# Softmax maxima in the score product: four rows spread by VectorE, or one row transposed per head and copied by ScalarE

## The chip, the cores and the metric

The kernel runs on one core of a Trainium2 chip, in float32 throughout. The time is the device time of one launch, in microseconds (us). Before the change three runs took 1527.92, 1532.71 and 1538.26 us; the median is 1532.71. "Faster" or "slower" is said against runs of the unchanged kernel on the same chip.

## The reference

Two layers over 1024 latent tokens (a grid of 16 rows by 64 columns) and 256 context tokens, width 1024. Layer 0 holds two attentions side by side, each with 8 query heads of width 64 that share 2 key/value heads: one global (every query sees the 256 context and 1024 latent keys), one windowed (context and latent keys at a distance of at most 128) with a learned sink logit per head. Layer 1 holds a convolution branch and a neighbourhood attention: 8 heads, each latent query sees the context and a window of 8 by 16 grid cells, with a table of biases. Gates, projections, norms and modulation stand around them. What matters here is the softmax:

```python
def gqa_attend(q, k, v, bias=None, sink=None):
    s = jnp.einsum("bqhgd,bkhd->bhgqk", q, k, preferred_element_type=jnp.float32) * ATTN_SCALE
    if bias is not None:
        s = s + bias
    if sink is not None:
        sink_col = jnp.broadcast_to(sink.astype(jnp.float32)[None, :, :, None, None], s.shape[:-1] + (1,))
        p = jax.nn.softmax(jnp.concatenate([s, sink_col], axis=-1), axis=-1)[..., :-1]
    else:
        p = jax.nn.softmax(s, axis=-1)
    return jnp.einsum("bhgqk,bkhd->bqhgd", p.astype(v.dtype), v)
```

## The kernel before

**Split numbers.** A float32 operand of a large product is held as a high part in the fast float32 format (`fp32r`) and a low part, the rest. A projection is three products (high by high, high by low, low by high; `mm3`, lines 351 to 354). The splitting is a cast on ScalarE (line 331) and a subtraction on GpSimd or VectorE (line 334).

**Attention by groups.** A group is 512 query columns: in layer 0 the four query heads of one key/value head for one block of 128 queries (40 groups, 20 of them windowed, with sinks), in layer 1 one head's 512 queries of half the grid, in four blocks of 128 (16 groups). Scores are computed with keys on the partitions and queries along the free axis, one tile of 128 keys by up to 512 queries at a time, into one of two PSUM banks `st`:

- line 529: keys' high and low parts (128 rows, `KA`) by the queries' high part, stored twice (`QH`);
- line 533: the keys' high part (64 rows of `KB`) by the queries' low part (64 rows of `QL`), and in the same contraction four more rows. Rows 64 to 67 of `KB` hold 1.0 (memset on GpSimd, lines 404 and 603). Rows 64 to 67 of `QL` hold minus the maximum of each query: row 64 + j has the values of head (or block) j in that head's 128 columns and zeros elsewhere. So the product subtracts each query's maximum from all its scores.

ScalarE then takes the exponential from the bank (line 541; in layer 1, where a bias is first added by VectorE in line 538, line 539), casts it to a high part (331), GpSimd or VectorE makes the low part (334), and three products per tile add up the values and the denominators in the bank `ov` (lines 480 to 482). These run three tiles behind the scores. For groups with a sink a last product (line 485) adds the sink's share of the denominator from further rows of `QL`.

**The maxima.** They are found ahead, with queries on the partitions: products `mx` (lines 643, 655, 663; in layer 1, 1405 and 1413) into one of two banks, each reduced by VectorE (645, 656, 664, 1407, 1414) into `mp`. `attn_prep` ends with `nmt`, 128 queries by 4 maxima; with a sink there are 12 columns: 4 maxima, and 4 high and 4 low parts of the sinks' exponentials (lines 433 to 446).

**The step of the change**, `attn_fin` (lines 450 to 461), brings `nmt` into `QL`. TensorE transposes it (line 457) into a bank `mx`, so that it is 4 (or 12) rows by 128 queries. VectorE (line 458) reads each row four times over, once for each head's columns, and multiplies by a constant matrix `bd` (12 by 4: −1 on the diagonal of the first four rows, +1 on those of the other eight), into rows 64 to 67 (or 75) of `QL`.

**What sets the order.** Each engine works through its own queue in order. The order is laid out when the program is built: the framework follows the order of the code with priorities and an estimated timeline (`schedule_with_timeline_sim=True`). The code is a set of generators: `attn_gen` yields between tiles, and while a group's tiles run, the next group's `attn_fin` and the preparation of the one after are stepped along (lines 507 to 515, 547 and 552). `weave` (line 562) puts steps of other work, projections of later heads and the output projections, between those steps. The transposition is pinned behind the last score product issued so far (`issue_after(sts[-1].ins)`, line 456). Bank `mx` is shared by turns: the transposition takes the next of the two, and the maxima's product two turns later must wait until the transposed rows have been read.

Of the kernel before, what the change touches and what calls it, by code (L numbers as in the profile page):

```python
# [10 lines left out]
F32 = mybir.dt.float32  # L11
F32R = mybir.dt.float32r
ALU = mybir.AluOpType
# [5 lines left out]
P = 128  # L19
# [70 lines left out]
def tile_kernel(ctx: ExitStack, tc: tile.TileContext, a, out):  # L90
# [14 lines left out]
    def bank(tag, name):  # L105
        if tag == "pp" and solo[0]:
            turn[0] += 1
            tag = ("pp", "mx")[turn[0] // 2 % 2]
        return ps.tile([P, 512], F32, tag=tag, name=name, bufs=BUFS[tag])
# [3 lines left out]
    def nm(s):  # L113
        uid[0] += 1
        return f"{s}_{uid[0]}"
# [5 lines left out]
    def const(name, shape, eng=SY, pool=None):  # L121
        t = (pool or cp).tile(shape, F32, tag=name, name=name)
        eng.dma_start(t, a[name])
        return t
# [265 lines left out]
        VE.scalar_tensor_tensor(dst, dst, 1.0, psrc, op0=ALU.add, op1=ALU.mult)  # L390


    bd = const("k_bd", [12, 4], SC)
    Ks, Vs = [], []

    def v_tiles(pool, n, bufs=1):
# [4 lines left out]
    def k_tiles(pool, hi, n, bufs=1):  # L401
        KB = pool.tile([P, n * P], F32R, tag="KB", name=nm("KBt"), bufs=bufs)
        KA = hi.tile([P, n * P], F32R, tag="KA", name=nm("KAt"), bufs=bufs)
        GP.memset(KB[64:68, :].bitcast(F32), 1.0)
        Ks.append((KA, KB))

    def load_k(k, kh, kl):
# [42 lines left out]
    def attn_fin(g):  # L450

        nr, nmt, QL = g.nr, g.nmt, g.QL
        for _ in range(FIN[layer[0]]):
            yield
        tr2 = bank("mx", nm("trn"))
        with tc.issue_after(sts[-1].ins) if sts else ExitStack():
            PE.transpose(tr2[0:nr, 0:P], nmt[:, 0:nr].bitcast(F32), ident)
        VE.tensor_tensor(QL[64 : 64 + nr, :].rearrange("p (h q) -> p h q", h=4),
                         tr2[0:nr, None, 0:P].broadcast_to([nr, 4, P]),
                         bd[0:nr, :, None].broadcast_to([nr, 4, P]), op=ALU.mult)  # L460
        yield

    def attn_gen(pool, groups, vshare, look, nexts=None):

        preps = [g.prep for g in groups]
        items = [(g, t) for g in groups for t in range(len(g.tiles))]
        pend = []
        cnt = [0]

        def flush():  # L470
            g, t, ph, pl = pend.pop(0)
            k, q0, n, _ = g.tiles[t]
            if t == 0:
                g.ov = bank("ov", nm("ov"))
                if g.load_v is not None:
                    g.load_v()
            V = g.v(k)
            last = t == len(g.tiles) - 1
            o = g.ov[:, q0 : q0 + n]
            PE.matmul(o, V[:, 64:192], ph[:, :n], start=(t == 0), stop=False)  # L480
            PE.matmul(g.ov[0:64, q0 : q0 + n], V[:, 0:64], ph[:, :n], start=False, stop=False)  # L481
            PE.matmul(o, V[:, 64:192], pl[:, :n], start=False, stop=(last and g.sink is None))  # L482
            if last:
                if g.sink is not None:
                    PE.matmul(g.ov, g.skm(), g.QL[0:76, :], start=False, stop=True)
                r1 = pool.tile([P, 8, 32], F32, tag="r1", name=nm("r1"), bufs=1)
                r8 = pool.tile([P, 8], F32, tag="r8", name=nm("r8"), bufs=2)
                rb = pool.tile([P, 256], F32, tag="rb", name=nm("rb"), bufs=1)
                for e in range(2):
                    VE.transpose(r1[e * 64 : (e + 1) * 64].rearrange("p a b -> p (a b)")  # L490
                                 .rearrange("p (a q) -> p a q", a=2), g.den(g.ov[64:128, :], e))
                VE.reciprocal(r8, r1[:, :, 0])
                VE.transpose(rb, r8[:, :, None].broadcast_to([P, 8, 32]))
                g.finish(g.ov, rb)

        if layer[0]:
            for g in groups[:3]:
                queries(g, kvs[-1])
        for p in preps[:2]:
            for n_, _ in enumerate(p):  # L500
                if n_ % 2:
                    yield
        for _ in attn_fin(groups[0]):
            pass
        if layer[0]:
            groups[0].copy()
        for gi, g in enumerate(groups):
            ids = [gi + 2] if gi + 2 < len(groups) else []
            if nexts is not None and gi in nexts:
                ids = nexts[gi]  # L510
            nx = [preps[k] for k in ids]
            if gi + 1 < len(groups):
                nx.insert(1 if ids[:1] == [gi + 1] else 0, attn_fin(groups[gi + 1]))
            g.next = chain.from_iterable(nx)
            g.step = -(-(18 * len(ids) + 4) // len(g.tiles))
        for g, t in items[:AHEAD]:
            g.ahead(t)
        for x, (g, t) in enumerate(items):
            if x + AHEAD < len(items):
                items[x + AHEAD][0].ahead(items[x + AHEAD][1])  # L520
            if t == 0:
                g.start()
                if layer[0] and g.no + 3 < len(groups):
                    queries(groups[g.no + 3], kvs[-1])
            k, q0, n, extra = g.tiles[t]
            KA, KB = g.k()
            st = bank("st", nm("st"))
            cs = slice(k * P, (k + 1) * P)
            sts.append(PE.matmul(st[:, :n], KA[:, cs], g.QH[:, q0 : q0 + n], start=True, stop=False))  # L529
            if not g.bias:  # L530
                for lhs, rhs in extra():
                    PE.matmul(st[:, :n], lhs, rhs, start=False, stop=False)
            PE.matmul(st[:, :n], KB[0:68, cs], g.QL[0:68, q0 : q0 + n], start=False, stop=True)  # L533
            ph = pool.tile([P, 512], F32R, tag="ph", name=nm("ph"), bufs=look + 1)
            pl = pool.tile([P, 512], F32R, tag="pl", name=nm("pl"), bufs=look + 1)
            pf = pool.tile([P, 512], F32, tag="pf" if layer[0] else "ost", name=nm("pf"), bufs=PFB)
            if g.bias and extra is not None:
                VE.tensor_tensor(pf[:, :n], st[:, :n], extra(), op=ALU.add)
                acts.append(SC.activation(pf[:, :n], pf[:, :n], AF.Exp))
            else:  # L540
                acts.append(SC.activation(pf[:, :n], st[:, :n], AF.Exp, scale=1.0 if g.bias else SCALE))  # L541
            cnt[0] += 1
            split(pf[:, :n], ph[:, :n], pl[:, :n], "s", "v" if cnt[0] % vshare == 0 else "g")
            pend.append((g, t, ph, pl))
            if t == len(g.tiles) // 2:
                g.gate()
            for _ in range(g.step // 2):
                next(g.next, None)
            yield
            if len(pend) > look:  # L550
                flush()
            for _ in range(g.step - g.step // 2):
                next(g.next, None)
            if t == len(g.tiles) - 1:
                for _ in g.next:
                    pass
            yield
        while pend:
            flush()
            yield  # L560
# [39 lines left out]
    def kv_tiles():  # L600

        KB = a0.tile([P, NTOK], F32R, tag="KB", name=nm("KBt"), bufs=1)
        GP.memset(KB[64:68, :].bitcast(F32), 1.0)
        for _ in range(2):
            KA = a0.tile([P, NTOK], F32R, tag="KA", name=nm("KAt"), bufs=2)
            V = a0.tile([P, 10, 192], F32R, tag="V", name=nm("Vt"), bufs=2)
            GP.memset(V[:, :, 128:192].bitcast(F32), 1.0)
            KV.append((KA, KB, V))
# [107 lines left out]
    with ExitStack() as p0x:  # L716
# [99 lines left out]
            VE.tensor_copy(gain5[:, 4, :], gain[:, 64:128])  # L816
            bmask = const("k_bm", [P, 384], SY, a0)
        bmt = a0.tile([P, 2, P], F32R, tag="bmt", name="bmt")
        sk = a0.tile([76, P], F32R, tag="sk", name="sk")
        cst = a0.tile([P, 512], F32, tag="ost", name="cst", bufs=2)  # L820
        with after_mod(4):
            SY.dma_start(cst[:, 0:256], a["k_bt"].rearrange("p a b -> p (a b)"))
            SY.dma_start(cst[0:76, 256:384], a["k_sk"])
        VE.tensor_copy(bmt, cst[:, 0:256].rearrange("p (a b) -> p a b", a=2))
        VE.tensor_copy(sk, cst[0:76, 256:384])

        tails = []
        beat = [0]
# [787 lines left out]
def _consts():  # L1616
# [16 lines left out]
    nxt = np.where(kk <= q, f(0), neg)  # L1633
    k["k_bm"] = np.concatenate([prev, z, nxt], 1).astype(f)
    k["k_bt"] = np.ascontiguousarray(np.stack([prev.T, nxt.T], 1)).astype(f)
    k["k_bd"] = np.where(np.arange(12)[:, None] < 4, f(-1), f(1)) * (np.arange(12)[:, None] % 4 == np.arange(4)[None, :])
    k["k_bd"] = k["k_bd"].astype(f)
    sk = np.zeros((76, 128), f)
    sk[68:76, 64:] = 1
    k["k_sk"] = sk  # L1640
    return k

# [92 lines left out]
```

## Time and profile before

| | |
|---|---|
| timed runs | 1527.92, 1532.71, 1538.26 us, median 1532.71 |
| span of the profiled execution, first to last instruction | 1528.5 us |
| TensorE products / weight loads busy | 1451.0 / 1167.2 us |
| VectorE / ScalarE / GpSimd busy | 1031.7 / 748.1 / 788.0 us |
| mean granted TensorE clock | 0.976 |
| instructions | 21545 |

The profiled execution is one more run; its own device time beyond its span is not recorded, and its span lies 4.2 us below the median of the timed runs. Its rows name an engine (PE is TensorE's products, PEld its weight loads, DVE VectorE, ACT ScalarE, POOL GpSimd, SP SyncE; a q behind it, as in ACTq, is the engine's sequencer, which issues DMAs), a line of the kernel, the operation, the tile written and the tiles read. In a row of one line or tile, the three numbers are the shortest, median and longest duration in ns, then the first and last start. In a row of order of time, the first number is the start in us, the second how long the run of equal instructions lasted, "x3" how many they are, and in brackets how long the engine had been idle and what released it. In a row of waits, the numbers are the total in us, how often, and the longest. In a row by stretches, each engine's busy time and its count of instructions follow, then the granted clock (1.00 is full), the share of the DMA engines' time and GB/s. Recorded ends of matrix products are modelled, and successive products overlap.

Layer 0's attention runs from about 146 to 886 us (windowed heads first), its output projection and the norms until 930, layer 1's convolution and projections to about 1200, its attention to 1476, the last projections and the norm to the end.

### The profile page before, as it was taken

How to read it: one execution, taken by the hardware profiler on the slowest of the kernel's cores; microseconds unless marked ns; L12 is line 12 of the kernel's file. 1: busy time of each engine (PE TensorE's matmuls, PEld its weight loads, DVE VectorE, ACT ScalarE, POOL GpSimd, SP SyncE). 2: the span in 40 equal slices, each digit the busy share in tenths (PEclk: the TensorE clock that was granted, in tenths of full speed). 3: DMA queues.
4: the chain of work that ended last, by engine and by line, in shares of the span. 5: the costliest groups of instructions: out<-in, count | busy, mean ns of one | idle time of the engine just before them, and what ended most of it. 6: DMA issues, size and time to landing. Idle time of an engine off the chain costs nothing.

```text
span 1528.5 us, 21545 instructions
## 1 busy us (share of the span) xinstructions
PE 1451.0 (95%) x7144; PEld 1167.2 (76%) x7144; DVE 1031.7 (67%) x2095; ACT 748.1 (49%) x1418; POOL 788.0 (52%) x628
## 2 busy tenths in 40 slices
PE   6999999998998999999999889999999999989996
PEld 2786877896896777886777568888887788868775
DVE  2643566589578856457676948899848666567766
ACT  3642433443435564447646665343334455455564
POOL 3360443555454766557645665665532434364665
PEclk9999999999999999999999999999999999989998
DMA  9564325422312246121202021210484677877642
GB/s 366 201 225 135 106 69 174 135 77 88 114 56 76 85 138 210 49 69 54 59 28 66 35 67 56 62 56 28 158 253 144 207 219 240 248 222 234 178 129 110
DMA packets 154167, 199.83 MB, mean 131 GB/s; under 512 B 14716, under 2 KB 95816, under 8 KB 154056
## 3 DMA queue, kind: packets, MB, share of 16 engines
q1 hardware_dynamic: 147392, 186.88, 38.9%
q10 hardware_dynamic: 6664, 11.57, 2.3%
q8 instruction: 56, 0.92, 0.3%
q14 instruction: 55, 0.45, 0.1%
HBM read 148.07 MB, written 49.02 MB: 129 GB/s over the span
## 4 chain that ended last, share of the span: by engine, by line
PE 79%; DVE 11%; issue 3%; DMA 3%; ACT 2%; POOL 1%; ACTq 0%; SPq 0%; DVEq 0%; POOLq 0%
PE p L352 6%; PE p L354 6%; PE p L353 6%; PE ov L480 5%; PE ov L482 4%; PE ov L481 4%; PE po L352 4%; PE st L533 4%; PE st L529 4%; PE po L353 4%; PE po L354 4%; PE pq L352 4%; PE pq L353 3%; PE pq L354 3%; PE pg L352 2%
## 5 line engine op out<-in xcount | busy, mean ns | idle before, releaser
L334 POOL TENSOR_TENSOR pl<-pf,ph 128x512 fp32r<-128x512 f32 (+4 forms) x321 | 394.0, 1239 | 384.9 <-ACT ph L331 337.3
L541 ACT ACTIVATE pf<-st 128x512 f32<-128x512 f32 x284 | 166.5, 597 | 203.6 <-PE st L533 165.2
L334 POOL TENSOR_TENSOR wl<-wr,wh 128x512 fp32r<-128x512 f32 (+2 forms) x131 | 169.3, 1302 | 136.5 <-ACT wh L331 124.0
L331 ACT CAST ph<-pf 128x512 fp32r<-128x512 f32 (+4 forms) x364 | 209.5, 588 | 27.1 <-PE ov L481 15.9
L352 PE MATMUL p<-hh,wh 128*128 128x512 f32 x448 | 176.0, 393 | 3.4 <-DVE spq L1233 1.3
L353 PE MATMUL p<-hl,wh 128*128 128x512 f32 x448 | 174.5, 390 | 0.0
L354 PE MATMUL p<-hh,wl 128*128 128x512 f32 x448 | 173.0, 391 | 0.0
L480 PE MATMUL ov<-ph,Vt 128*128 128x512 f32 (+4 forms) x364 | 141.0, 387 | 4.2 <-DVE y L693 2.0
L529 PE MATMUL st<-QH,KAt 128*128 128x512 f32 (+4 forms) x364 | 140.2, 386 | 3.9 <-ACT pf L541 3.1
L482 PE MATMUL ov<-pl,Vt 128*128 128x512 f32 (+4 forms) x364 | 141.1, 388 | 2.2 <-POOL pl L334 2.1
L481 PE MATMUL ov<-ph,Vt 128*64 128x512 f32 (+4 forms) x364 | 138.9, 381 | 0.0
L533 PE MATMUL st<-QL,KBt 68*128 68x512 f32 (+4 forms) x364 | 136.4, 386 | 0.9 <-issue 0.8
L1177 DVE SCALAR_TENSOR_TENSOR cps<-U,taps,cps 128x512 f32<-128x512 f32 x184 | 125.9, 748 | 0.7
L331 ACT CAST wh<-wr 128x512 fp32r<-128x512 f32 (+2 forms) x134 | 80.9, 613 | 84.1 <-PE po L353 15.9
L352 PEld LDWEIGHTS p<-hh,wh 128*128 128x128 f32 x448 | 84.2, 188 | 21.5 <-ACT spq L1231 1.6
L656 DVE TENSOR_REDUCE mp<-mx 128x1 f32<-128x512 f32 x128 | 85.3, 681 | 19.3 <-PE mx L655 18.3
L354 PEld LDWEIGHTS p<-hh,wl 128*128 128x128 f32 x448 | 84.1, 188 | 17.4
L353 PEld LDWEIGHTS p<-hl,wh 128*128 128x128 f32 x448 | 84.2, 188 | 17.1 <-issue 0.2
L1020 DVE SCALAR_TENSOR_TENSOR x<-po,modT,x 128x512 f32<-128x512 f32 (+1 forms) x72 | 46.9, 657 | 64.0 <-PE po L354 63.5
L352 PE MATMUL pq<-wh,hh 128*128 128x384 f32 x256 | 88.2, 344 | 1.0 <-ACT hh L331 1.0
L353 PE MATMUL pq<-wl,hh 128*128 128x384 f32 x256 | 87.3, 341 | 0.0
L354 PE MATMUL pq<-wh,hl 128*128 128x384 f32 x256 | 86.6, 342 | 0.0
(287 smaller groups left out, 3417.2 us busy)
## 6 DMA issues: line engine op xcount, KB each, us to landing
mw<-in_mod_w_dram SPq DMA_DIRECT2D x16, 1024.0 KB, 5.3
Q<-qs SPq DMA_DIRECT2D x40, 256.0 KB, 2.1
QH<-Q SPq DMA_DIRECT2D x80, 128.0 KB, 2.7
mw<-in_mod_w_dram SPq DMA_DIRECT2D x16, 512.0 KB, 6.8
wr<-in_od_d_dram SPq DMA_DIRECT2D x32, 256.0 KB, 3.1
wr<-in_ev_qkv_dram SPq DMA_DIRECT2D x16, 384.0 KB, 5.0
KAt<-KD SPq DMA_DIRECT2D x16, 384.0 KB, 6.5
wr<-in_od_wo_dram SPq DMA_DIRECT2D x22, 256.0 KB, 3.4
```

The lines of the kernel that those rows point to most:

```text
L331: acts.append(SC.copy(hi, src))
L334: (GP if leng == "g" else VE).tensor_tensor(lo, src, hi.bitcast(F32), op=ALU.subtract)
L352: PE.matmul(o, lh, rh, start=first, stop=False)
L353: PE.matmul(o, lh, rl, start=False, stop=False)
L354: last.append(PE.matmul(o, ll, rh, start=False, stop=end))
L480: PE.matmul(o, V[:, 64:192], ph[:, :n], start=(t == 0), stop=False)
L481: PE.matmul(g.ov[0:64, q0 : q0 + n], V[:, 0:64], ph[:, :n], start=False, stop=False)
L482: PE.matmul(o, V[:, 64:192], pl[:, :n], start=False, stop=(last and g.sink is None))
L529: sts.append(PE.matmul(st[:, :n], KA[:, cs], g.QH[:, q0 : q0 + n], start=True, stop=False))
L533: PE.matmul(st[:, :n], KB[0:68, cs], g.QL[0:68, q0 : q0 + n], start=False, stop=True)
L541: acts.append(SC.activation(pf[:, :n], st[:, :n], AF.Exp, scale=1.0 if g.bias else SCALE))
L1177: VE.scalar_tensor_tensor(pc, uc, w, pc, op0=ALU.mult, op1=ALU.add)
```

## The change

The maxima enter line 533 as one row: `KB` has a single row of −1.0 and `QL` a single row with all 512 maxima. To get them into one row, the four heads (or blocks) are transposed one at a time: four transpositions, each of the one column of `nmt` that belongs to the head (with a sink of three columns: maximum, high and low part of the sink's exponential, a step of four apart), each into its own 128 columns of the same bank. ScalarE copies the result, 1 row (or 3) by 512, into row 64 (or rows 64 to 66) of `QL`. The constant matrix and its DMA are gone; line 533 contracts over 65 rows, line 485 over 67, and the sink's constant matrix has 67 rows. All four transpositions are pinned behind the last score product, as the one was.

```diff
-    bd = const("k_bd", [12, 4], SC)
     Ks, Vs = [], []
...
     def k_tiles(pool, hi, n, bufs=1):
         KB = pool.tile([P, n * P], F32R, tag="KB", name=nm("KBt"), bufs=bufs)
         KA = hi.tile([P, n * P], F32R, tag="KA", name=nm("KAt"), bufs=bufs)
-        GP.memset(KB[64:68, :].bitcast(F32), 1.0)
+        GP.memset(KB[64:65, :].bitcast(F32), -1.0)
...
         tr2 = bank("mx", nm("trn"))
+        nr //= 4
         with tc.issue_after(sts[-1].ins) if sts else ExitStack():
-            PE.transpose(tr2[0:nr, 0:P], nmt[:, 0:nr].bitcast(F32), ident)
-        VE.tensor_tensor(QL[64 : 64 + nr, :].rearrange("p (h q) -> p h q", h=4),
-                         tr2[0:nr, None, 0:P].broadcast_to([nr, 4, P]),
-                         bd[0:nr, :, None].broadcast_to([nr, 4, P]), op=ALU.mult)
+            for h_ in range(4):
+                PE.transpose(tr2[0:nr, h_ * P : (h_ + 1) * P],
+                             nmt.rearrange("p (j h) -> p j h", h=4)[:, 0:nr, h_].bitcast(F32), ident)
+        SC.copy(QL[64 : 64 + nr, :], tr2[0:nr, :])
         yield
...
                 if g.sink is not None:
-                    PE.matmul(g.ov, g.skm(), g.QL[0:76, :], start=False, stop=True)
+                    PE.matmul(g.ov, g.skm(), g.QL[0:67, :], start=False, stop=True)
...
-            PE.matmul(st[:, :n], KB[0:68, cs], g.QL[0:68, q0 : q0 + n], start=False, stop=True)
+            PE.matmul(st[:, :n], KB[0:65, cs], g.QL[0:65, q0 : q0 + n], start=False, stop=True)
...
     def kv_tiles():
 
         KB = a0.tile([P, NTOK], F32R, tag="KB", name=nm("KBt"), bufs=1)
-        GP.memset(KB[64:68, :].bitcast(F32), 1.0)
+        GP.memset(KB[64:65, :].bitcast(F32), -1.0)
...
-        sk = a0.tile([76, P], F32R, tag="sk", name="sk")
+        sk = a0.tile([67, P], F32R, tag="sk", name="sk")
...
-            SY.dma_start(cst[0:76, 256:384], a["k_sk"])
+            SY.dma_start(cst[0:67, 256:384], a["k_sk"])
...
-        VE.tensor_copy(sk, cst[0:76, 256:384])
+        VE.tensor_copy(sk, cst[0:67, 256:384])
...
-    k["k_bd"] = np.where(np.arange(12)[:, None] < 4, f(-1), f(1)) * (np.arange(12)[:, None] % 4 == np.arange(4)[None, :])
-    k["k_bd"] = k["k_bd"].astype(f)
-    sk = np.zeros((76, 128), f)
-    sk[68:76, 64:] = 1
+    sk = np.zeros((67, 128), f)
+    sk[65:67, 64:] = 1
     k["k_sk"] = sk
```

## The prediction

> **What bounds the kernel now.** I read the page first: its busy line and its chain of waits.
>
> ```profile
> span 1528.5 us, 21545 instructions
> ...
> PE 1451.0 (95%) x7144; PEld 1167.2 (76%) x7144; DVE 1031.7 (67%) x2095; ACT 748.1 (49%) x1418; POOL 788.0 (52%) x628
> ...
> PE 79%; DVE 11%; issue 3%; DMA 3%; ACT 2%; POOL 1%; ACTq 0%; SPq 0%; DVEq 0%; POOLq 0%
> ```
>
> TensorE is busy 95% of the span, and 79% of the chain that ended last is its own work; only 11% is VectorE, 2% ScalarE. That is an average over stages, so I then asked for the busy time in the three stretches in which the changed step runs: the two halves of layer 0's attention (windowed heads, then global ones) and layer 1's attention.
>
> ```profile
> core 0: us, PE busy (x) PEld busy (x) DVE busy (x) ACT busy (x) POOL busy (x), PEclk, DMA share, GB/s
> 146.00:491.00 345.00, 335.08 (x1727) 281.30 (x1723) 236.70 (x559) 147.43 (x312) 165.37 (x123) 0.99 0.31 98
> 491.00:886.00 395.00, 377.39 (x1742) 291.43 (x1742) 266.40 (x475) 227.62 (x405) 242.70 (x184) 0.98 0.25 79
> 1198.00:1476.00 278.00, 267.67 (x1344) 220.98 (x1345) 190.78 (x445) 151.52 (x298) 138.67 (x127) 0.98 0.74 217
> ```
>
> Together 1018 us, with TensorE busy in 980.1, VectorE in 693.9 (68%), ScalarE in 526.6 (52%). So in these stages TensorE's own stream sets the pace: work added to it lengthens the span nearly one for one, unless it falls into the 37.9 us in which it stands. Work taken off VectorE pays only where TensorE stands for VectorE.
>
> The changed step itself, from the query on the tile that the transposition writes:
>
> ```profile
> L457 PE MATMUL trn<-ident,nmt x56: 269/272/382, 146.4 to 1474.9; 128*4 128x128 f32 x36, 128*12 128x128 f32 x20
> L458 DVE TENSOR_TENSOR QL<-trn,k_bd x56: 671/682/685, 147.2 to 1475.5; 4x512 fp32r<-4x512 f32 x36, 12x512 fp32r<-12x512 f32 x20
> ...
>   DVE QL L458: 42.5, 23
>   PEld mx L643: 3.5, 4
>   PE mx L643: 1.8, 3
> ```
>
> It happens 56 times, once per group of four heads or four query blocks: one transposition, one spread of 682 ns. The last lines say who waited: VectorE stood 42.5 us, in 23 places, for the transposition, and TensorE's products for the maxima stood a few times for the spread, because the transposition borrows one of the two banks of those products.
>
> **Term 1: three more transpositions per group, 168 in all.** The recorded 272 ns is mostly latency; what counts is by how much the next start is put off. Two rows tell it: a run of three transpositions elsewhere, and the order of starts around one of the 56.
>
> ```profile
> 69.57 0.49 PE L932 MATMUL trk<-ident,pc 128*128 128x128 f32 x3
> ...
> L932 PE MATMUL trk<-ident,pc x120: 270/272/329, 69.6 to 542.3; 128*128 128x128 f32 x120
> ```
>
> Three in a row cover 0.49 us and one lasts 0.272, so each start is (0.49 − 0.272) / 2 = 0.109 us after the one before.
>
> ```profile
> 566.00 0.40 PE L533 MATMUL st<-QL,KBt 68*128 68x512 f32 x1
> 566.24 0.27 PE L457 MATMUL trn<-ident,nmt 128*4 128x128 f32 x1
> 566.26 0.48 PE L643 MATMUL mx<-KAt,QH 128*128 128x256 f32 x2
> 566.58 0.40 PE L529 MATMUL st<-QH,KAt 128*128 128x512 f32 x1
> 566.82 0.39 PE L533 MATMUL st<-QL,KBt 68*128 68x512 f32 x1
> ```
>
> A product of 512 columns is followed after 0.24 us (566.00 to 566.24, 566.58 to 566.82); from the first of them to the second there are 0.58 us. In between lie one such product, two of 256 columns (together as many columns, so about the same) and the transposition: 0.58 − 2 × 0.24 = 0.10 us. Both ways give 0.1 although one loads 128 columns of weights and the other 4. What remains unseen is four transpositions with one or three columns in a row. The weight loads bound that:
>
> ```profile
> L457 PEld LDWEIGHTS trn<-ident,nmt x56: 81/85/89, 146.2 to 1474.7; 128*4 128x4 f32 x36, 128*12 128x12 f32 x20
> ...
> L932 PEld LDWEIGHTS trk<-ident,pc x120: 137/140/146, 69.4 to 542.1; 128*128 128x128 f32 x120
> ```
>
> If the load set the pace in the run of three, a load shorter by 55 ns would bring 0.109 down to about 0.054, and 168 of them would cost 9.1 us. I take 0.109, because the transposition with the short load cost no less: 168 × 0.109 = 18.3 us. By the other reading, 0.10, it is 16.8; the upper end, with 0.11 for rounding, is 18.5.
>
> The Trainium skill ("TensorE: Matmul & The Clock Gate", sections "Wait — 56ns, not 53.3ns?" and "Back-to-back issue gap") puts warm starts at 128 columns about 56 ns apart, or about 81 ns in a stream with weight loads; by these the term would be 9.3 or 13.6 us. This trace's float32 transpositions are at 109 ns and do not agree.
>
> **Term 2: what VectorE gives back.** 56 × 0.682 = 38.2 us of VectorE work go. What it is worth is on the chain of waits, where the spread is a piece of its own at six places (the first and the last are shown):
>
> ```profile
> 147.22 0.69 DVE QL L458
> ...
> 1415.56 0.69 DVE QL L458
> ```
>
> Six times 0.69 is 4.1 us, which I take as the gain; it may be nothing where the bank then waits for ScalarE. It may be more if other waits shrink with VectorE's load (the first rival).
>
> **Term 3: 56 copies on ScalarE.** The copy out of PSUM has 1 or 3 rows of 512; nearest is one of 128 rows.
>
> ```profile
> L234 ACT COPY mrow<-pm x8: 579/587/588, 72.4 to 357.3; 128x512 f32<-128x512 f32 x8
> ...
> ACT pf L541 <- PE st L533: 165.2, 100, 12.1
> ```
>
> 56 × 0.587 = 32.9 us, which lifts ScalarE from 52% to 55% of those stages. Rows hardly matter: the spread takes 671 to 685 ns, though 36 of the 56 have 4 rows and 20 have 12. What stands behind the copy in ScalarE's order are the exponentials (line 541) and the casts after them, and TensorE's value products wait for those. But the exponentials stood 165.2 us in 100 places for TensorE's scores: ScalarE runs ahead of it. I take 0, with the second rival as the price if that cover is gone. The copy's own readers are far behind:
>
> ```profile
> L533 PE MATMUL st<-QL,KBt 68*128 68x512 f32 (+4 forms) x364 | 136.4, 386 | 0.9 <-issue 0.8
> ```
>
> Line 533 reads the row, and none of its 0.9 us of idle time is put down to the spread. So a later copy costs nothing there; the bank is held perhaps 0.33 us longer by the transpositions and about 0.1 us less by the faster copy, which is inside term 2's range.
>
> **The small edits.** Line 533 contracts over 65 rows in place of 68 and line 485 over 67 in place of 76; the columns set the spacing (lines 529 with 128 rows and 533 with 68 are both followed after 0.24 us above), so nothing. The memsets of one row in place of four run on GpSimd a handful of times. One DMA issue leaves ScalarE's queue at the start:
>
> ```profile
> 0.72 0.63 ACTq L123 DMA_DIRECT2D k_bd<-in_k_bd_dram  x1
> ...
> 5.66 0.42 ACT L767 ACTIVATE acc<-xr 128x256 f32<-128x256 f32 x1 [2.37 <-DMA xr<-in_cT_dram]
> ```
>
> ScalarE stands 2.37 us for the context's DMA afterwards, so its 0.63 us were covered: nothing. Last, the order on each engine is laid out by estimated times when the program is built, so new instructions can move their neighbours. No row prices that. I bound it, either way, by a quarter of the 37.9 us in which TensorE stands: 9 us.
>
> **The sum.** 18.3 − 4.1 = +14.2 us, on the profiled 1528.5 a span of 1542.7. The three timed runs lie at 1527.92 to 1538.26 around 1532.71; on that median, 1532.7 + 14.2 = 1546.9, taken as 1547, +0.93%. About 1% is what a measurement of this kernel can tell from no change, so this sits just below the edge (1548.0).
>
> **Rivals.** *VectorE is the hidden bound of the maxima* (the other side). TensorE's largest waits for VectorE around this step are
>
> ```profile
> PE mx L655 <- DVE mp L656: 7.8, 14, 1.9
> PE trn L457 <- DVE nmt L436: 2.5, 3, 1.0
> PE trn L457 <- DVE nmt L446: 2.1, 3, 1.3
> PE ov L480 <- DVE y L693: 2.0, 6, 0.6
> PE mx L643 <- DVE QL L458: 1.8, 3, 1.1
> PE mx L655 <- DVE mp L645: 1.8, 3, 0.9
> ```
>
> together 18.0 us, and after long ones the granted clock is low for a while:
>
> ```profile
> 373.00:382.00 9.00, 8.52 (x27) 6.44 (x28) 8.15 (x19) 3.73 (x9) 3.46 (x3) 0.62 0.18 60
> 472.00:477.00 5.00, 4.82 (x18) 3.95 (x19) 3.13 (x7) 1.82 (x5) 1.36 (x2) 0.66 0.01 3
> 797.00:801.00 4.00, 4.00 (x13) 3.03 (x12) 3.47 (x6) 2.24 (x5) 2.69 (x2) 0.57 0.10 28
> 868.00:876.00 8.00, 5.78 (x13) 3.18 (x14) 7.89 (x11) 5.87 (x12) 7.88 (x6) 0.57 0.00 0
> ```
>
> At 0.62, 0.66, 0.57 and 0.57 these stretches lose (1 − clock) × length: 3.4 + 1.7 + 1.7 + 3.4 = 10.2 us. All of it gone gives 1532.7 + 18.3 − 18.0 − 10.2 = 1522.8. For it: all these waits are near the spread. Against: one instruction of 682 ns in a group rarely carries a whole wait. It decides for "not slower" once the waits returned exceed 18.3 us; chance 0.12, half of it over 1% faster.
>
> *ScalarE takes over the standing.* The 23 waits of 42.5 us, 1.85 each, move to ScalarE with exponentials behind them. Score tiles have two banks and a tile is five products, so about 2 × 5 × 0.24 = 2.4 us of TensorE work cover a stand; some will find it used up. If a third of the places (8) pay 1.85 us, +14.8: 1561.7. Against it speak the 165.2 us of slack. Chance 0.2.
>
> *Short transpositions follow each other faster*, at 0.054: +9.1 − 4.1 = +5.0, 1537.7, no difference that can be told. The skill's figures above lean this way, the rows at 0.10 and 0.109 against. Chance 0.2.
>
> **How the numbers follow.** Forecast 0.45, 1547 with ±8 for the order: 0.21 of it above 1548.0, 0.24 within 1%. ScalarE's standing, 0.2: slower but for 0.01. Short transpositions, 0.2: within 1% but for 0.02 slower. VectorE's rival, 0.12: half faster, half same. An order that outweighs everything, 0.03: 0.01 faster, 0.02 same. Sum: slower 0.42, same 0.51, faster 0.07. The range runs from 1530 (short transpositions less 8 of order) to 1563 (ScalarE's standing); it leaves out most of the first rival and the worst of the second.
>
> **What the profile after would show.** TensorE has 168 more products, starts inside a group of transpositions are 0.11 us apart, and its busy time grows by about 18 us in the three stretches; VectorE's falls by 38 and ScalarE's rises by 33; the spread's pieces are gone from the chain. I am wrong if the starts are near 0.05, if score products wait for exponentials by many microseconds more than now, or if TensorE's waits for VectorE's maxima fall by ten or more.

## The result, and the profile after

The changed kernel takes 1544.57 us (median of 6 runs, 1540.54 to 1548.16) beside 1533.23 us for the kernel before (6 runs, 1527.92 to 1538.26): a ratio of 1.0078 with a 95% interval of 1.0056 to 1.0101. So it is slower by 11 to 12 us (11.3 between the medians, 12.0 by the ratio), under the 1% that the prediction called the edge, and inside its range (1547, 1530 to 1563).

The head of the page of the changed kernel:

```profile
span 1538.8 us, 21867 instructions
...
PE 1463.3 (95%) x7312; PEld 1175.0 (76%) x7312; DVE 990.0 (64%) x2039; ACT 782.2 (51%) x1474; POOL 789.8 (51%) x628
...
PE 79%; DVE 9%; DMA 4%; issue 3%; POOL 2%; ACT 2%; SPq 0%; ACTq 0%; DVEq 0%; POOLq 0%
```

The span grew by 10.3 us. The counts say that the change does what it says: 168 more products, 56 fewer instructions on VectorE, 56 more on ScalarE. VectorE's busy time fell by 41.7 us and ScalarE's rose by 34.1; VectorE's share of the chain fell from 11% to 9%. TensorE's busy time rose by 12.3 us. The prediction had it rise by about 18 us in the three stretches of attention. In the same three windows the changed kernel has

```profile
sum 1018.00, PE 985.94 PEld 797.06 DVE 644.99 ACT 548.91 POOL 537.82; mean PE 328.65 PEld 265.69 DVE 215.00 ACT 182.97 POOL 179.27
```

which is 5.8 us more for TensorE, 48.9 less for VectorE (38 were forecast) and 22.3 more for ScalarE (33 were forecast), so TensorE's sign did not come as said. The windows do not cut the work at the same places, though: the first transposition starts 2.3 us later than before (148.7 against 146.4), the last 8.3 us later (1483.2 against 1474.9). The 2.3 us lie ahead of the step at issue.

The rows of the transposition's tile, and the order of starts on TensorE around one group:

```profile
L458 PEld LDWEIGHTS trn<-ident,nmt x224: 79/83/88, 148.5 to 1483.1; 128*1 128x1 f32 x72, 128*3 128x3 f32 x40
L458 PE MATMUL trn<-ident,nmt x224: 270/272/275, 148.7 to 1483.2; 128*1 128x128 f32 x72, 128*3 128x128 f32 x40
L460 ACT CAST QL<-trn x56: 572/574/577, 149.7 to 1484.4; 1x512 fp32r<-1x512 f32 x36, 3x512 fp32r<-3x512 f32 x20
...
  ACT QL L460: 31.7, 19
...
  PEld mx L643: 1.6, 3
  PE mx L643: 0.9, 2
```

```profile
562.71 0.40 PE L481 MATMUL ov<-ph,Vt 128*64 128x512 f32 x1
562.95 0.60 PE L458 MATMUL trn<-ident,nmt 128*1 128x128 f32 x4
563.30 0.48 PE L643 MATMUL mx<-KAt,QH 128*128 128x256 f32 x2
563.62 0.40 PE L482 MATMUL ov<-pl,Vt 128*128 128x512 f32 x1
```

Four transpositions cover 0.60 us and one lasts 0.272: (0.60 − 0.272) / 3 = 0.109 us from start to start, with one column of weights. By the prediction's other way there are 0.91 us from 562.71 to 563.62; less 2 × 0.24 for the products of 512 columns, 0.43 us are left for four transpositions, where one had 0.10. That is 0.33 us more in a group, 18.5 us in 56 of them. The copy takes 574 ns where the prediction took 587. ScalarE now stands 31.7 us in 19 places for the transpositions, where VectorE stood 42.5 us in 23. TensorE waits less for the bank than before (0.9 us and, in layer 1, 0.2; 1.8 before).

The rows of TensorE's waits that answer to the six of the prediction, and the granted clock of the two kernels, before first:

```profile
PE mx L655 <- DVE mp L656: 6.1, 13, 1.5
PE trn L458 <- DVE nmt L445: 4.1, 3, 2.4
PE ov L480 <- DVE y L693: 3.1, 7, 0.8
PE st L529 <- ACT pf L541: 2.8, 8, 0.7
...
PE mx L655 <- DVE mp L645: 1.7, 1, 1.7
...
PE mx L643 <- ACT QL L460: 0.9, 2, 0.4
...
PE trn L458 <- DVE nmt L435: 0.2, 1, 0.2
```

```profile
core 0: 1528.5 us, clock 0.976
```

```profile
core 0: 1538.8 us, clock 0.981
```

The six were 18.0 us and are 16.1 (6.1 + 4.1 + 3.1 + 1.7 + 0.9 + 0.2), 1.9 less. The clock took (1 − 0.976) × 1528.5 = 36.7 us before and (1 − 0.981) × 1538.8 = 29.2 us after, 7.5 less. With 18.3 us for the starts that makes 18.3 − 1.9 − 7.5 = +8.9 of the span's +10.3.

The 7.5 us belong to the two executions that were profiled, and not to the change. The profiled run of the changed kernel is the fastest of its six, whose clocks go from 0.973 to 0.981 with a mean of 0.977; the kernel before, in its runs beside the experiments, has means of 0.975 to 0.978 on three chips, and single runs from 0.969 to 0.984. How a stretch of low clock comes and goes is seen at one place: TensorE stands 1.43 us (in brackets) for the same product in the kernel before (first row) and in the changed one (second row); the third row is the changed kernel's stretch behind it.

```profile
373.19 0.52 PE L932 MATMUL trk<-ident,pc 128*128 128x128 f32 x3 [1.43 <-DVE KAt L334]
```

```profile
375.04 0.52 PE L932 MATMUL trk<-ident,pc 128*128 128x128 f32 x3 [1.43 <-DVE KAt L334]
```

```profile
375.00:384.00 9.00, 8.94 (x46) 7.23 (x46) 4.87 (x14) 4.50 (x11) 1.71 (x2) 1.00 0.21 75
```

Behind it the clock was 0.62 before (373 to 382 us, shown in the prediction) and is 1.00 now (375 to 384): the stand has the same length, the clock is another. Without the term of the clock, 18.3 − 1.9 = 16.4 us stand beside the 11 to 12 measured, and what makes up the difference is not shown.

The wait for the exponentials (line 541) is 2.8 us, 3.1 before: ScalarE's copy did not hold TensorE up.

In the chain of waits no piece of VectorE's spread is left; the step now shows up there as short links, as here:

```profile
463.87 1.45 DVE nmt L445
...
465.36 0.62 PE trn L458 x4
...
466.00 0.58 ACT QL L460
...
466.62 0.53 PE mx L643 x2
```

### The profile page after: what moved, and what is told of

It is laid out like the page before. It is cut to its first block, busy times and chain, and to the rows that moved or that the text cites. A ratio compares the mean times of both kernels' runs of the same rounds, so it can differ in the third digit from the quotient of the medians.

```text
span 1538.8 us, 21867 instructions
## 1 busy us (share of the span) xinstructions
PE 1463.3 (95%) x7312; PEld 1175.0 (76%) x7312; DVE 990.0 (64%) x2039; ACT 782.2 (51%) x1474; POOL 789.8 (51%) x628
## 4 chain that ended last, share of the span: by engine, by line
PE 79%; DVE 9%; DMA 4%; issue 3%; POOL 2%; ACT 2%; SPq 0%; ACTq 0%; DVEq 0%; POOLq 0%
PE p L352 6%; PE p L354 6%; PE p L353 6%; PE ov L480 4%; PE ov L482 4%; PE ov L481 4%; PE po L352 4%; PE po L353 4%; PE po L354 4%; PE st L529 4%; PE st L533 4%; PE pq L354 3%; PE pq L353 3%; PE pq L352 3%; PE pg L352 2%
## 5 line engine op out<-in xcount | busy, mean ns | idle before, releaser
L541 ACT ACTIVATE pf<-st 128x512 f32<-128x512 f32 x284 | 166.4, 596 | 163.2 <-PE st L533 127.1
L533 PE MATMUL st<-QL,KBt 65*128 65x512 f32 (+4 forms) x364 | 136.1, 385 | 0.9 <-issue 0.8
L645 DVE TENSOR_REDUCE mp<-mx 128x2 f32<-128x512 f32 x80 | 55.0, 690 | 83.2 <-PE mx L643 82.7
L353 PEld LDWEIGHTS p<-hl,wh 128*128 128x128 f32 x448 | 84.2, 188 | 16.9 <-issue 0.2
L529 PEld LDWEIGHTS st<-QH,KAt 128*128 128x128 f32 x364 | 69.1, 190 | 23.9 <-ACT pf L541 9.8
```

The costliest lines, as they stand in the source:

```text
L353: PE.matmul(o, lh, rl, start=False, stop=False)
L533: PE.matmul(st[:, :n], KB[0:65, cs], g.QL[0:65, q0 : q0 + n], start=False, stop=True)
```

## The experiments

Every ratio is against runs of the kernel before on the same chip, and a difference in us is worked out from the ratio unless medians are named.

**Four transpositions, VectorE's spread kept** (the added TensorE work alone):

```diff
-            PE.transpose(tr2[0:nr, 0:P], nmt[:, 0:nr].bitcast(F32), ident)
+            for h_ in range(4):
+                PE.transpose(tr2[0:nr, h_ * P : (h_ + 1) * P], nmt[:, 0:nr].bitcast(F32), ident)
```

> The kernel before, with three more transpositions of the same maxima per group, into columns of the bank that nobody reads; VectorE's spread stays, ScalarE gets no copy. Theory A (the change costs 168 starts of 0.109 us on TensorE, and VectorE's freed 38 us gave about 7 us back): here only the cost, +18.3, so 1551.5 us (1547 to 1555), TensorE's starts 0.109 us apart. Theory B (the transpositions fell partly into time in which TensorE stands anyway, and VectorE's freed time gave nothing): the same as the changed kernel, 1544 to 1546.

Measured: 1560.45 us against 1530.28, ratio 1.0194 (1.0170 to 1.0217), +29.7 us. That is far more than 18.3, and more than the changed kernel. Neither theory had it. Part of it goes with the clock: the mean of its five runs is 0.972, that of 17 runs of the kernel before on this chip 0.978. VectorE's wait for the transposition in this kernel:

```profile
DVE QL L459 <- PE trn L458: 48.4, 28, 4.7
```

It stood 48.4 us where it stood 42.5 before.

**The changed kernel with the copy on VectorE:**

```diff
-        SC.copy(QL[64 : 64 + nr, :], tr2[0:nr, :])
+        VE.tensor_copy(QL[64 : 64 + nr, :], tr2[0:nr, :])
```

> The changed kernel with its copy of 1 or 3 rows done by VectorE in place of ScalarE, so that only the engine of the copy differs. Theory A: VectorE keeps 56 instructions of about 0.65 us, so what it gave back is gone: 1550 us (1546 to 1554). Theory B: the same as the changed kernel within 2 us, 1543 to 1547.

Measured: 1570.12 us, ratio 1.0243 (1.0216 to 1.0271), +37.2 us. Theory B falls, and theory A's 1550 us are missed by 20. The changed kernel differs from this one in the engine of the copy alone, and it stands 1.65%, some 25 us, below it. The instructions of VectorE, in the kernel with four transpositions and the spread and in this one:

```profile
L459 DVE TENSOR_TENSOR QL<-trn,k_bd x56: 672/682/684, 149.0 to 1502.7; 4x512 fp32r<-4x512 f32 x36, 12x512 fp32r<-12x512 f32 x20
```

```profile
L460 DVE CAST QL<-trn x56: 671/682/684, 149.4 to 1516.0; 1x512 fp32r<-1x512 f32 x36, 3x512 fp32r<-3x512 f32 x20
```

So this kernel and the previous experiment do the same work in the step (four transpositions and one VectorE instruction of 682 ns per group), and 7.5 us lie between them. What differs is the number of rows and of weight columns (both smaller here) and the order in which the program was laid out. That it is the order is argued and not shown. So a third theory was needed: order itself may be worth as much as the terms at issue.

**The transpositions as products in the fast float32 format**, in the changed kernel:

```diff
-                PE.transpose(tr2[0:nr, h_ * P : (h_ + 1) * P],
-                             nmt.rearrange("p (j h) -> p j h", h=4)[:, 0:nr, h_].bitcast(F32), ident)
+                PE.matmul(tr2[0:nr, h_ * P : (h_ + 1) * P],
+                          nmt.rearrange("p (j h) -> p j h", h=4)[:, 0:nr, h_], identr, start=True, stop=True)
```

> The changed kernel with the four transpositions written as products in the fast float32 format: one column of maxima as weights, the identity as the moving operand (the maxima are of that format already, so the values are the same). If the 128 moving columns set the 0.109 us, at two passes for float32, one pass halves it: starts about 0.055 us apart, 168 x 0.054 = 9.1 us less than the changed kernel, 1535.5 us. If something fixed per transposition sets it (weight load, dispatch), starts stay at 0.109 and the time at 1544.6.

Measured: 1546.44 us, ratio 1.0101 (1.0079 to 1.0124), so not faster than the changed kernel (1.0078). The starts did come closer:

```profile
574.61 0.41 PE L458 MATMUL trn<-ident,nmt 128*1 128x128 f32 x4
```

```profile
L458 PE MATMUL trn<-ident,nmt x224: 218/222/308, 150.0 to 1491.3; 128*1 128x128 f32 x72, 128*3 128x128 f32 x40
```

(0.41 − 0.222) / 3 = 0.063 us, which should have saved 168 × (0.109 − 0.063) = 7.7 us. In the profiled execution TensorE's largest wait for VectorE's maxima and the clock stand against it:

```profile
PE mx L655 <- DVE mp L656: 10.1, 13, 3.5
```

```profile
core 0: 1547.9 us, clock 0.975
```

The wait is 10.1 us against 6.1, and the clock takes (1 − 0.975) × 1547.9 = 38.7 us against 29.2. Over all six runs of each kernel the mean clocks are 0.975 and 0.977, some 39 and 35 us, so the profiled pair overstates the clock's part, and what ate the saving is not shown in full. Within a run of transpositions, then, the cost of a start goes by the format in which they are written, not quite by half, and the time did not follow it. That float32 takes two passes is not shown.

**The same in the kernel before**, one product in the fast format for its one transposition:

```diff
-            PE.transpose(tr2[0:nr, 0:P], nmt[:, 0:nr].bitcast(F32), ident)
+            PE.matmul(tr2[0:nr, 0:P], nmt[:, 0:nr], identr, start=True, stop=True)
```

> The kernel before with its one transposition per group as a product in the fast float32 format. If the moving columns alone set what one costs, 56 x 0.054 = 3.0 us less: 1530.2 us. If the weight load of the product behind it (128 columns, which a short product can't hide) sets it, nothing: 1533.2 us.

Measured: 1526.99 us (12 runs) against 1530.28 (17 runs), ratio 0.9979 (0.9966 to 0.9993), −3.2 us, where 3.0 was worked out. It is the fastest of all kernels here. But its trace does not show the saving:

```profile
153.84 0.40 PE L533 MATMUL st<-QL,KBt 68*128 68x512 f32 x1
154.08 0.23 PE L457 MATMUL trn<-ident,nmt 128*12 128x128 f32 x1
154.14 0.45 PE L643 MATMUL mx<-KAt,QH 128*128 128x256 f32 x2
154.43 0.39 PE L480 MATMUL ov<-ph,Vt 128*128 128x512 f32 x1
```

From 153.84 to 154.43 there are 0.59 us; less 2 × 0.24, 0.11 us are left for the one product in the fast format, no less than the 0.10 of the float32 transposition in the kernel before. So a single transposition between large products gains nothing by the format, as the second side of the expectation has it (whether by the weight load behind it is not shown). Its products also run in another order than those of the kernel before, so the agreement of −3.2 with 3.0 is luck.

**VectorE's working time put back, without a wait:**

```diff
+    scr = cp.tile([4, 8], F32, tag="scr", name="scr")
...
         SC.copy(QL[64 : 64 + nr, :], tr2[0:nr, :])
+        VE.tensor_reduce(scr[0:4, 0:1], one[0:4, 0:1].broadcast_to([4, 512]), axis=AX.X, op=ALU.max)
```

> The changed kernel with 56 more instructions of VectorE, one behind each copy: a reduction over 512 elements of a constant, about 0.6 us, which waits for nothing and which nobody reads. Theory W (VectorE's freed working time is what gave time back against four transpositions with VectorE's spread): most of it is lost, 1552 to 1560 us beside about 1542 to 1545 for the changed kernel. Theory Q (what gave time back is that VectorE's queue no longer stands for the transpositions): within 3 us of the changed kernel.

Measured: 1551.44 us, ratio 1.0138 (1.0110 to 1.0165). The run does not test what it was meant to, as the rows of its scratch tile show:

```profile
L462 DVE TENSOR_REDUCE scr<-one x56: 658/674/675, 0.9 to 53.6; 4x1 f32<-4x512 f32 x56
```

All 56 ran between 0.9 and 53.6 us: nothing bound them to their place, and they were laid out at the front. There they may have put off the rest: the first transposition starts at 154.0 us, in the changed kernel at 148.7. The run is inconclusive.

**VectorE's wait put back, without work:**

```diff
+    scr = cp.tile([4, 8], F32, tag="scr", name="scr")
...
+        VE.tensor_copy(scr[0:nr, 0:1], tr2[0:nr, 511:512])
         SC.copy(QL[64 : 64 + nr, :], tr2[0:nr, :])
```

> The changed kernel with 56 tiny instructions of VectorE (one column of the transposed rows into a scratch tile that nobody reads): almost no work, but VectorE's queue stands for the four transpositions again. Theory W: within 4 us of the changed kernel. Theory Q: towards four transpositions with VectorE's spread (1560), at least 1552 us.

Measured: 1558.37 us, ratio 1.0181 (1.0154 to 1.0208), as theory Q had it. The waits, however, show a second thing that came with it:

```profile
DVE scr L461 <- PE trn L459: 59.3, 31, 5.1
ACT QL L462 <- DVE scr L461: 55.7, 27, 8.6
```

VectorE stands 59.3 us again, but ScalarE's copy now also stands 55.7 us for VectorE's read of the same bank. So the run can't say which of the two, or the new order, costs the 16 us by which it stands above the changed kernel. Its mean clock is lower too, 0.970 against 0.977.

**Order alone.** The kernel before, with one constant of its ordering changed, and the changed kernel with the same:

```diff
-LATE = 100
+LATE = 120
```

> The kernel before with one constant of its ordering changed (the priority offset of the modulation's steps from 100 to 120): the same instructions in another order, 1961 lines of the order on TensorE differ. It shows how much the order alone is worth. If order is a small term (within 3 us), 1528 to 1533 us. If it is as large as the terms at issue, 6 us or more away from 1530.

> The changed kernel with the same constant changed. If the change costs the same in any order, this stands 0.6 to 1.0% above the kernel before with that constant. If the measured 0.78% is mostly an accident of the order, the difference is below 0.3% or above 1.3%.

Measured: the kernel before 1546.98 us, ratio 1.0110 (1.0078 to 1.0141), +16.9 us (14.3 between the medians) with not one instruction of work added; the changed kernel 1560.93 us, ratio 1.0195 (1.0166 to 1.0224), 0.85% above its partner. The page of the reordered kernel before, its transposition and its clock:

```profile
span 1552.5 us, 21536 instructions
...
PE 1467.7 (95%) x7144; PEld 1171.5 (75%) x7144; DVE 1035.1 (67%) x2095; ACT 749.2 (48%) x1418; POOL 790.1 (51%) x628
```

```profile
L457 PE MATMUL trn<-ident,nmt x56: 269/272/278, 158.7 to 1499.5; 128*4 128x128 f32 x36, 128*12 128x128 f32 x20
```

```profile
core 0: 1552.5 us, clock 0.974
```

The same 7144 products keep TensorE "busy" 16.7 us longer; the clock accounts for (1 − 0.974) × 1552.5 − 36.7 = 3.7 us of it. The first transposition starts 12.3 us later (158.7 against 146.4), ahead of all attention, the last 24.6 us later (1499.5 against 1474.9): half of the profiled loss of 24.0 us lies before the step at issue has run once, half is spread behind it.

**A third order**, and four transpositions with VectorE's spread in the second and the third:

```diff
-FL = (80, -98)
+FL = (84, -98)
```

> The kernel before with another constant of its ordering changed (the priority offset of the woven work in layer 0 from 80 to 84): the same instructions in a third order. From the first change of order, which cost 14 us, anything from 1526 to 1550 us.

> The changed kernel with that constant. If the cost of the change is the same in any order, 0.7 to 1.0% above the kernel before with that constant (11 to 15 us), as in the two orders so far (0.78 and 0.9%). If the order rules, outside of 0.3 to 1.4%.

> Four transpositions with VectorE's spread (the idle three more) with that constant. If the idle transpositions cost only their starts, 18.3 us above the kernel before with that constant, and moving the copy to ScalarE is worth 4 to 6 us. If VectorE's longer standing in its queue is a real cost, 25 to 30 us above it, as in the first order.

> The same with the constant of the modulation's steps at 120. If the idle transpositions cost only their starts, 1.2% above the kernel before with that constant, so 2.3% above the kernel before as it stands (1565 to 1569 us). If VectorE's standing is a real cost, 2.8 to 3.1% above it (1573 to 1580).

Measured, as ratios to the kernel before as it stands:

| order | before | four, VectorE's spread | changed | changed − before | four − before | changed − four |
|---|---|---|---|---|---|---|
| as it stands | 1 | 1.0194 | 1.0078 | +0.78% | +1.94% | −1.16% |
| LATE 120 | 1.0110 | 1.0207 | 1.0195 | +0.85% | +0.97% | −0.12% |
| FL 84 | 1.0031 | 1.0158 | 1.0140 | +1.09% | +1.27% | −0.18% |

Each ratio's interval is 0.2 to 0.3% to either side (four with LATE 120: 1.0184 to 1.0229; with FL 84: 1.0135 to 1.0182; changed with FL 84: 1.0116 to 1.0164; before with FL 84: 1.0013 to 1.0048), so a difference of two is known to 0.3 to 0.4%. Four with LATE 120 ran on another chip than its two partners. At 1533 us the cost of the change is 12, 13 and 17 us, 14 in the mean. Three idle transpositions cost 30, 15 and 19 us, 21 in the mean. The four transpositions with a copy on ScalarE come 18, 2 and 3 us below those with VectorE's spread; the two small ones can't be told from nothing. Of the two forecasts for four transpositions with the spread in the new orders, that of the starts alone came out (15 and 19 us above the kernel before in the same order, 18.3 said), that of a real cost of VectorE's standing (25 to 30 us, or 2.8 to 3.1%) in neither. The changed kernel with FL 84 (1.09%) lies between its two forecasts.

A part of what is left between the orders goes with the clock. The mean clocks of the runs are 0.977 for the changed kernel and 0.972 for four transpositions as it stands; 0.976, 0.973 and 0.976 with LATE 120 (before, changed, four); 0.975, 0.972 and 0.972 with FL 84. From run to run of one kernel, each us more of (1 − clock) × span goes with about half a us of time (0.52, over 130 runs of all these kernels). As an estimate, that share of the loss taken out of each kernel's mean time leaves 14, 11 and 14 us for the change, 24, 17 and 18 for the idle transpositions, and 11, 6 and 4 for what the copy on ScalarE saves against the spread. So a part of the 30 us of the first order goes with the clock; why less of it was granted there is not shown.

## Why the prediction was right

*TensorE sets the pace, term 1.* Right. The start-to-start time of 0.109 us came out exactly, with one column of weights as with 128. It costs about what was said: idle transpositions alone cost 21 us in the mean of three orders (15 to 30), with 18.3 worked out. The rival of short starts falls for float32 transpositions. The Trainium skill ("TensorE: Matmul & The Clock Gate", section "Wait — 56ns, not 53.3ns?") has about 56 ns between warm starts at 128 columns. Here the fast format came near it within a run of four (63 ns), float32 transpositions did not (109 ns).

*Term 2, VectorE gives 4.1 us back.* The sum came out (14.2 worked out, 14 measured in the mean of three orders), but the way that the prediction gave for this term is not shown. It counted the six pieces of the spread on the chain. In the profiled pair TensorE's waits shrank by 1.9 us, and the 7.5 us of clock beside them are an accident of the two executions. Against four transpositions with VectorE's spread, the copy on ScalarE was worth 18 us in the order as it stands and 2 to 3 us, within an error of about 5, in the two others; with the clock's share taken out the estimate is 11, 6 and 4. So a return of some us is likely, and its size and its way stay open.

*Term 3, ScalarE's copies cost nothing.* Right. They are 32 us of work (56 of 574 ns), the exponentials still stood 127.1 us for TensorE's scores, and TensorE's wait for exponentials did not grow:

```profile
  PE st L533: 127.1, 98
```

The rival by which ScalarE takes over the standing falls: its 31.7 us did not reach TensorE. *The first rival* (VectorE as the hidden bound) falls too: six waits lost 1.9 us of their 18.0, where it wanted them all, and over its six runs the mean clock of the changed kernel (0.977) is that of the kernel before (0.975 to 0.978).

*The small edits* left no trace that can be told apart. *The order* was the mis-sized term: bounded by 9 us from the time in which TensorE stands, it measured 16.9 (14.3 between the medians) in one neutral change and 4.8 (0.31%) in another. The bound was wrong in kind: the larger loss began before attention and showed partly as longer "busy" time; that short stands hide in that is likely and not shown. That the sum fits to 2 or 3 us in the order as it stands is therefore partly chance; that it fits in the mean of three orders is the better support.

What stays open: whether the larger part of VectorE's return comes from its working time or from its standing in its queue, why four transpositions with VectorE's spread cost 30 us in one order and 15 in another, and where the 7.7 us that the fast format saves on TensorE's starts went.

## What to carry to other kernels

On a path that TensorE's stream sets, count small products by the time from start to start and not by their recorded length, and look for that number in a run of equal products elsewhere in the same trace; what a less busy engine gives back may be small beside it, and here it went with the order. The clock of one profiled execution is not the kernel's: take it over several runs before a difference is put down to it. Where a program's order is laid out from estimated times, a difference of 1% between two versions is no more than a neutral change of order makes: time both versions in two or three orders before the cause of it is told. An operation of an experiment that depends on nothing will not stay where it is written; bind it to its place.

## What was not expected of the hardware and the program

In a run of float32 transpositions with 128 moving columns the starts are 0.109 us apart, whether the weights have 1, 3, 4, 12 or 128 columns, and those of the same products in the fast format 0.063 us. Yet a single one between large products takes up 0.10 to 0.11 us in either format. And a kernel in which TensorE is busy 95% of the time can lose 14 to 17 us to order alone, with the same instructions.
